# Mean squares of seven attention and recurrent heads, summed along the free axis with tokens on partitions

## The chip, the core and the metric

The kernel runs on one core of a Trainium2 chip. The metric is the device time of one execution in microseconds (us). Beside the times there is one profiled execution, taken by the hardware profiler. Its engines are PE (TensorE's matmuls; PEld are its weight loads), DVE (VectorE), ACT (ScalarE), POOL (GpSimd) and SP (which issues transfers). L96 is line 96 of the kernel before.

## The reference, cut to what matters

One layer of an encoder trunk on 512 tokens of width 1024, in float32: a norm, one wide input projection, three branches (pooling, differential attention with four heads, a bidirectional gated recurrence with four heads), gates, an output projection, a second norm, a SwiGLU feed-forward network (FFN) of 2816 hidden columns, a final norm. The change lies where a head's output, 512 tokens by 128 channels, is normalised:

```python
def rms_norm(x, g):
    y = xf * lax.rsqrt(jnp.mean(xf * xf, axis=-1, keepdims=True) + NORM_EPS)
    return (y * g).astype(x.dtype)
# attention, each of 4 heads
o = rms_norm(o, gain) * (1.0 - lambda_init)
# recurrence, each of 4 heads
o = rms_norm((o_f + o_b), gain).reshape(B, S, REC_WIDTH)
return o * jax.nn.silu(g)
```

The mean goes over a head's 128 channels, so there is one factor per token and head.

## The kernel before

**Arithmetic.** Products of float32 tensors are made from two parts each, a rounded one ("hi", fp32r) and its remainder ("lo"), as hi x hi + hi x lo + lo x hi. `split_w` (L185) makes the parts of a weight tile: ScalarE writes whi, VectorE wlo. The recurrence and the norms use plain float32 matmuls, which TensorE runs as two passes each; transposes (L104) take one.

**Stages.** The input is normalised and transposed to hT (channels on partitions, tokens along the free axis). Then come the recurrent heads, the attention heads, the gates and branch projections, the output projection, the FFN, and the last output product, which is made of plain products and of seven block products.

**Order.** The order of TensorE's instructions is written out by a planner, `Pipe` (L39). Every head is a stream (`rec_scan`, `att_head`), and one further stream, `jobs`, holds the projections. A stream yields ("w", t, slack): what follows it is to be issued no earlier than t us on the planner's own clock, which every matmul moves on by a fixed price (L93 to L105). Meanwhile the other streams' matmuls are issued. TensorE takes its instructions in that order and waits when an input isn't ready. The orders of the other engines are chosen by the framework from its own estimate of time.

**A head's norm.** Heads are worked with channels on partitions: o_ps in PSUM is 128 channels x 512 tokens. `head_norm` (L692 to L717) squares it on ScalarE (sqo, L697), copies it scaled by the gain (og, L698), and after a wait of 1.3 us takes the sum over partitions on TensorE: four float32 matmuls with a block of sqo as the stationary operand and one column of 1/128 as the moving one (L702), which leaves 128 tokens x 4 in PSUM. VectorE adds the epsilon (L153; attention, whose outputs are not yet divided by their softmax sums, multiplies by r0 twice before, L708 to L710), GpSimd raises to the power -0.5 (L147). After a further wait of 3.55 us four transposes of the broadcast column (L716) turn the factor back to the form of og, and VectorE multiplies (L1014 or L1160). A recurrent head also multiplies by its silu gate sg (L1013). The result is split into y_hi and y_lo. Tiles in PSUM come from two or three buffers for each of the names mm, rc and tp.

**Layout.** SBUF is given out by pools, one behind the other from the left: const, wraw (raw weights), wsp (the split weights whi and wlo, slots of 4352 bytes in each partition, 17 x 256), small, and then hTp with hT and all later pools: the attention tiles, the forms (sums of input blocks for products with fewer multiplications), h2 (the second norm's hT), the FFN's tiles wss (split sums shi and slo) and lw. The y arenas and a few others come from the right end. `small` reserves five slots of 32 bytes for each of its names: ss, rstd, ms, rso, mx, co, mo and ss2, 1280 bytes in all. Its end is where hT begins. The code places tiles by small distances: h2 stands behind a pad of 192 bytes (L1816), lw too (L1846), and `split_w` has a skip, by which whi and wlo begin 64 or 192 bytes into their slot:

```python
hi, lo = ((wpool or wsp).tile([P, n if wpool else 1088], F32R, name=name)[:, k:k + n]
```

Weights of 512-column products have no skip (but for a few branch projections, where it is 64), those of the gate pairs and of the first three fronts 64, and those of the value projections, where whi is the moving operand and hT the stationary one, 192. The FFN works in column pairs, seven products of 12 passes each with 256 columns; three take whi and four take shi.

Of the kernel before, what the change touches and what calls it, by code (L numbers as in the profile page):

```python
# [11 lines left out]
F32 = mybir.dt.float32  # L12
F32R = mybir.dt.float32r
U8 = mybir.dt.uint8
AF = mybir.ActivationFunctionType
ALU = mybir.AluOpType
PSUM = bass.MemoryType.PSUM

P = 128
S = 512  # L20
D = 1024
NB = S // P
KT = D // P
HEADS = 4
FFN = 2816
FT = FFN // P
EPS = 1e-6
# [55 lines left out]
def encoder_kernel(ctx: ExitStack, tc: tile.TileContext, x, norm1_g, w_in, pool_w, pool_scale,  # L83
# [3 lines left out]
    nc = tc.nc  # L87
# [7 lines left out]
    def mm(out_, lhsT, rhs, start, stop, chain=False):  # L95
        i = nc.tensor.matmul(out_, lhsT=lhsT, rhs=rhs, start=start, stop=stop, skip_group_check=chain)  # L96
        tc.keep_in_program_order(i)
        n = 1
        for d in rhs.shape[1:]:
            n *= d  # L100
        pipe.t += max(0.107, n * 0.0004167 + 0.002) if rhs.dtype == F32R else max(0.216, n * 0.001667 + 0.004)

    def transpose(out_, in_, idn):
        tc.keep_in_program_order(nc.tensor.transpose(out_, in_, idn))  # L104
        pipe.t += 0.108  # L105
# [11 lines left out]
    small = ctx.enter_context(pool("small", 5))  # L117
    psum = ctx.enter_context(pool("psum", 3, space=PSUM))

    def bank(name, shape=(P, 512)):  # L120
        return psum.tile(list(shape), F32, name=name, bufs=2 if name == "tp" else 3)
# [7 lines left out]
    ident = const.tile([P, P], F32, name="ident")  # L129
    make_identity(nc, ident)  # L130
    fixed = const.tile([P, 2], F32, name="fixed")
    onesD, minus1 = fixed[:, 0:1], fixed[:, 1:2]
    nc.vector.memset(onesD, 1.0 / P)
    nc.vector.memset(minus1, -1.0)
    mhalf = const.tile([P, 8], F32, name="mhalf")
    nc.vector.memset(mhalf, -0.5)
# [2 lines left out]
    gain_a = const.tile([P, 1], F32, name="gain_a")  # L139
# [4 lines left out]
    gain_r = vcol[:, 13:14]  # L144

    def pow_mhalf(dst, src):
        return nc.gpsimd.tensor_tensor(out=dst, in0=src, in1=mhalf[:, :src.shape[1]], op=ALU.pow).ins  # L147

    def rsqrt_eps(dst, mean):

        ms = small.tile([P, 8], F32, name="ms")[:, :mean.shape[1]]
        eng = nc.vector if mean.space == PSUM else nc.gpsimd
        eng.tensor_scalar(out=ms, in0=mean, scalar1=1.0, scalar2=EPS, op0=ALU.mult, op1=ALU.add)  # L153
        return pow_mhalf(dst, ms)

    LAST, FF = {}, {}
# [434 lines left out]
    ps = bank("mm")  # L591
# [13 lines left out]
    ps = bank("mm")  # L605
# [17 lines left out]
    last = first_split((on_act, on_dve))  # L623
# [65 lines left out]
        nc.vector.tensor_copy(out=masks, in_=maskf)  # L689
    st0.close()  # L690

    def head_norm(o_ps, tmp, gain, r0=None, bufs=2, slack=0.0):  # L692


        og = tmp.tile([P, S], F32, name="og", bufs=bufs)
        sq = tmp.tile([P, S], F32, name="sqo", bufs=bufs)
        nc.scalar.activation(out=sq, in_=o_ps, func=AF.Square)  # L697
        nc.scalar.activation(out=og, in_=o_ps, func=AF.Copy, scale=gain)  # L698
        yield ("w", 1.3, slack)
        sp = bank("tp")  # L700
        for b in range(NB):
            mm(sp[:, b:b + 1], sq[:, b * P:(b + 1) * P], onesD, True, True)  # L702
        r = small.tile([P, NB], F32, name="rso")
        if r0 is None:
            rsqrt_eps(r, sp[:, 0:NB])
        else:
            m = small.tile([P, NB], F32, name="mo")
            nc.vector.tensor_tensor(out=m, in0=sp[:, 0:NB], in1=r0, op=ALU.mult)  # L708
            nc.vector.tensor_tensor(out=m, in0=m, in1=r0, op=ALU.mult)
            nc.vector.tensor_scalar(out=m, in0=m, scalar1=EPS, scalar2=None, op0=ALU.add)  # L710
            pow_mhalf(r, m)
            nc.vector.tensor_tensor(out=r, in0=r, in1=r0, op=ALU.mult)
        yield ("w", 3.55, slack)
        rb = bank("tp")
        for b in range(NB):
            transpose(rb[:, b * P:(b + 1) * P], r[:, b:b + 1].to_broadcast([P, P]), ident)  # L716
        return og, rb  # L717
# [195 lines left out]
    def rec_scan(h):  # L913
# [30 lines left out]
        n = 1  # L944
# [54 lines left out]
                nc.vector.scalar_tensor_tensor(out=own, in0=st[:, 3 * d + prev, :], scalar=total, in1=ps[:, j, :],  # L999
                                               op0=ALU.mult, op1=ALU.add)  # L1000
        yield ("w", 2.4 if h < 3 else 1.6, slack)
        ps = bank("rc")
        for b in range(NB):
            o = ps[:, b * P:(b + 1) * P]
            mm(o, vs[b], pt[:, b, :], True, False)
            for d in range(2):
                if 0 <= b - 1 + 2 * d < NB:
                    j = b - 1 if d == 0 else b
                    mm(o, st[:, 3 * d + j, :], kq[:, 1 - d, b * P:(b + 1) * P], False, b == (0 if d else 3) or d == 1)
        mark(f"O{h}")  # L1010
        og, rbp = yield from head_norm(ps, rt, gain_r, slack=slack)
        yield ("e", f"G{h}", 0.0)
        nc.vector.tensor_tensor(out=og, in0=og, in1=sgs.pop(h), op=ALU.mult)  # L1013
        nc.vector.tensor_tensor(out=og, in0=og, in1=rbp, op=ALU.mult)  # L1014
        nc.scalar.copy(out=y_rec[0][:, h, :], in_=og)
        nc.vector.tensor_tensor(out=y_rec[1][:, h, :], in0=og, in1=y_rec[0][:, h, :].bitcast(F32), op=ALU.subtract)

# [72 lines left out]
    def att_head(h):  # L1090
        if h:
            yield ("e", f"QK{h - 1}", 0.0)
        yield ("e", f"AF{h}", 7.0 if h > 1 else 6.0)
        t = att.pop(h)
        at, (vh, vl), aT, y_attn = ATT["at"], ATT["v"], ATT["aT"], ATT["y"]
        strip = ATT["strip"].tile([P, 896], F32, name="strip")
        nc.sync.dma_start(out=strip, in_=c_dist[h])
        zz = at.tile([P, NB, 2], F32, name="zz")
        rr = at.tile([P, NB], F32, name="rr")
        probs = {}  # L1100

        def scores(i):
            bs = slice(i * P, (i + 1) * P)
            mx = small.tile([P, 2], F32, name="mx")
            ex = []
            for c in range(2):
                ps = bank("rc")
                mm(ps, t[f"q{c}"][:, bs], t[f"k{c}"], True, False)
                mm(ps, t[f"q{c}"][:, bs], t[f"l{c}"], False, True)
                s = at.tile([P, S], F32, name=f"s{c}")  # L1110

                nc.vector.tensor_tensor_reduce(out=s, in0=strip[:, 384 - P * i:896 - P * i], in1=ps, scale=1.0,  # L1112
                                               scalar=3.0e38, op0=ALU.add, op1=ALU.min, accum_out=mx[:, c:c + 1])
                nc.scalar.activation(out=s, in_=s, func=AF.Exp, scale=-1.0, bias=mx[:, c:c + 1],  # L1114
                                     accum_out=zz[:, i, c:c + 1])
                ex.append(s)

            co = small.tile([P, 2], F32, name="co")
            zn, co = co[:, 0:1], co[:, 1:2]
            nc.gpsimd.tensor_tensor(out=zn, in0=zz[:, i, 0:1], in1=nlam, op=ALU.mult)  # L1120
            nc.gpsimd.tensor_tensor(out=co, in0=zz[:, i, 1:2], in1=minus1, op=ALU.pow)
            nc.gpsimd.tensor_tensor(out=co, in0=co, in1=zn, op=ALU.mult)
            nc.vector.scalar_tensor_tensor(out=ex[0], in0=ex[1], scalar=co, in1=ex[0], op0=ALU.mult, op1=ALU.add)
            probs[i] = ex[0]

        def turn(i):
            bs = slice(i * P, (i + 1) * P)
            p = probs.pop(i)
            pt = bank("tp", (P, NB, P))
            for k in range(NB):  # L1130
                transpose(pt[:, k, :], p[:, k * P:(k + 1) * P], ident)
            nc.scalar.copy(out=aT[0][:, :, bs], in_=pt)
            nc.vector.tensor_tensor(out=aT[1][:, :, bs], in0=pt, in1=aT[0][:, :, bs].bitcast(F32), op=ALU.subtract)

        scores(0)
        for i in range(NB):
            yield ("w", 1.6 + (0.7 if i == 0 else 0.0))
            if i + 1 < NB:
                scores(i + 1)
            else:  # L1140
                mark(f"QK{h}")
            yield ("w", 2.4 + (1.0 if i + h == 0 else 0.0), 0.0)
            if h and i == 0:
                yield ("e", f"PV{h - 1}", 0.0)
            turn(i)
        mark(f"T{h}")
        nc.vector.reciprocal(out=rr, in_=zz[:, :, 0])
        yield ("e", "VA", 1.5)
        yield ("w", 1.5)
        ps = bank("rc")  # L1150
        es = slice(h * P, (h + 1) * P)
        terms = [(vh, aT[0]), (vl, aT[0]), (vh, aT[1])]
        for i, (a, r) in enumerate(terms):
            for k in range(NB):
                mm(ps, a[:, k, es], r[:, k, :], i == 0 and k == 0, i == 2 and k == NB - 1)
            yield
        mark(f"PV{h}")
        og, rbp = yield from head_norm(ps, at, gain_a, rr, 1, 6.0 if h < HEADS - 1 else 0.0)
        mark(f"AN{h}")
        nc.vector.tensor_tensor(out=og, in0=og, in1=rbp, op=ALU.mult)  # L1160
        nc.scalar.copy(out=y_attn[0][:, h, :], in_=og)
        nc.vector.tensor_tensor(out=y_attn[1][:, h, :], in0=og, in1=y_attn[0][:, h, :].bitcast(F32),
                                op=ALU.subtract)
# [733 lines left out]
```

## Time and profile before

| | us |
|---|---|
| median of 3 runs | 871.92 (871.59 to 872.09) |
| the profiled execution, its own time | 871.81 |
| its span, first to last instruction | 870.0 |
| TensorE matmuls busy | 862.4 |
| TensorE weight loads busy | 786.1 |
| VectorE busy | 659.2 |
| ScalarE busy | 448.7 |
| GpSimd busy | 37.1 |

How to read the rows of the profile: a group's row gives line, engine, operation, output<-inputs by the program's names, shape, xcount, then busy time and mean ns of one, then idle time of the engine before it and what ended it. Matmuls are pipelined, so that a pass's own duration is longer than the distance to the next; the pace is read from starts. A timeline row gives start, length, engine, line, operation and count; a row of the chain of waits gives start, length, engine, output, line and count; a row by windows gives the stretch, its length, then busy time and count of PE, PEld, DVE, ACT and POOL, the granted clock, the share and rate of transfers.

### The profile page before, as it was taken

Reading aid. Unit: us, or ns where it says so; the run is one execution under the profiler, and the core shown is the slowest. Engines: PE = TensorE matmul, PEld = TensorE weight load, DVE = VectorE, ACT = ScalarE, POOL = GpSimd, SP = SyncE. Lnnn points to the kernel's source line nnn. Section 1 sums busy time; section 2 is a strip of 40 time slices with the busy share of each in tenths; the row PEclk is TensorE's granted clock in tenths of the full one; section 3 lists DMA queues with packets and bytes.
Section 4 is the critical chain, followed back from the end, with each engine's and each line's share of the span. In section 5 each row is a group of like instructions: output and inputs, shape, how many; then the busy total and the mean of one; then the engine's idle time right before and its main releaser. Section 6 shows DMA issues by size and latency. Waiting matters only on the chain.

```text
span 870.0 us, 14113 instructions
## 1 busy us (share of the span) xinstructions
PE 862.4 (99%) x5713; PEld 786.1 (90%) x5713; DVE 659.2 (76%) x979; ACT 448.7 (52%) x721; POOL 37.1 (4%) x83
## 2 busy tenths in 40 slices
PE   9999999999999999999999999999999999999997
PEld 8989998888988888899999998999999999988886
DVE  6779644845757888987776756988888888847996
ACT  6644343435757664563354425655555655533563
POOL 2000000000102220000000001000000000000001
PEclk9999999999999999999999999999999999999999
DMA  8330113024133321343332840344433433355002
GB/s 245 98 122 25 50 49 121 25 74 151 43 95 90 90 68 49 97 146 98 97 98 97 288 124 1 85 112 128 114 98 108 136 98 99 121 194 192 2 1 98
DMA packets 115694, 87.54 MB, mean 101 GB/s; under 512 B 3862, under 2 KB 104748, under 8 KB 115628
## 3 DMA queue, kind: packets, MB, share of 16 engines
q1 hardware_dynamic: 115036, 85.57, 32.2%
q8 instruction: 45, 0.74, 0.4%
q10 hardware_dynamic: 592, 1.05, 0.3%
q14 instruction: 21, 0.17, 0.1%
HBM read 84.52 MB, written 2.10 MB: 100 GB/s over the span
## 4 chain that ended last, share of the span: by engine, by line
PE 98%; issue 1%; DMA 0%; DVE 0%; POOL 0%; ACT 0%; POOLq 0%
PE mm L96 65%; PE rc L96 28%; PE tp L96 3%; PE tp L104 2%; DMA xin<-in_x_dram 0%; PE rc L104 0%; DVE hrow L502 0%; POOL rstd L147 0%; ACT silu L1479 0%; ACT x L1503 0%; DVE x L1472 0%; DVE x L1481 0%; PE mm L104 0%; POOLq L1892 0%; POOL ms L153 0%
## 5 line engine op out<-in xcount | busy, mean ns | idle before, releaser
L191 ACT CAST whi<-raw 128x1024 fp32r<-128x1024 f32 (+1 forms) x134 | 127.5, 959 | 140.7 <-PE mm L96 95.2
L192 DVE TENSOR_TENSOR wlo<-raw,whi 128x1024 fp32r<-128x1024 f32 (+1 forms) x134 | 147.8, 1106 | 50.9 <-ACT whi L191 41.3
L96 PE MATMUL mm<-hT_hi,whi 128*128 128x512 f32 (+1 forms) x344 | 81.3, 370 | 0.0
L96 PE MATMUL mm<-hT_hi,wlo 128*128 128x512 f32 (+1 forms) x344 | 80.0, 368 | 0.0
L96 PE MATMUL mm<-hT_lo,whi 128*128 128x512 f32 (+1 forms) x344 | 78.8, 367 | 0.0
L96 PEld LDWEIGHTS mm<-hT_hi,whi 128*128 128x128 f32 x344 | 59.2, 188 | 10.3 <-ACT hT_hi L515 0.2
L96 PEld LDWEIGHTS mm<-hT_lo,whi 128*128 128x128 f32 x344 | 59.1, 188 | 9.8
L96 PEld LDWEIGHTS mm<-hT_hi,wlo 128*128 128x128 f32 x344 | 58.8, 188 | 9.5
L318 DVE TENSOR_TENSOR slo<-sums,shi 128x1024 fp32r<-128x1024 f32 x54 | 65.7, 1217 | 0.0
L316 ACT CAST shi<-sums 128x1024 fp32r<-128x1024 f32 x54 | 56.8, 1052 | 4.1 <-DVE sums L280 3.3
L276 DVE TENSOR_TENSOR sums<-raw 128x1024 f32<-128x1024 f32 x27 | 32.9, 1218 | 1.2 <-DMA raw<-in_w_in_dram 1.2
L96 PE MATMUL mm<-y_arena,whi 128*128 128x512 f32 x128 | 32.7, 394 | 0.0
L96 PE MATMUL mm<-whi,y_arena 128*128 128x256 f32 (+1 forms) x192 | 32.1, 317 | 0.0
L96 PE MATMUL rc<-kq,kc 128*128 128x128 f32 x224 | 30.4, 284 | 0.0
L96 PEld LDWEIGHTS rc<-kq,kc 128*128 128x128 f32 x224 | 29.2, 191 | 1.1
L961 DVE TENSOR_TENSOR kq<-kq,pyr 128x256 f32<-128x256 f32 x48 | 18.2, 420 | 15.8 <-PE rc L96 15.8
L96 PEld LDWEIGHTS mm<-whi,y_arena 128*128 128x128 f32 x192 | 27.9, 189 | 2.6
L929 ACT COPY kc<-kq 128x512 f32<-128x512 f32 x28 | 18.6, 667 | 21.6 <-DVE kq L955 8.2
L1114 ACT ACTIVATE s<-s,mx 128x512 f32<-128x512 f32 x32 | 23.0, 719 | 10.9 <-DVE mx L1112 10.2
L96 PEld LDWEIGHTS mm<-y_arena,whi 128*128 128x128 f32 x128 | 23.7, 188 | 5.1
L1413 DVE TENSOR_TENSOR g<-mm,g 128x256 f32<-128x256 f32 x21 | 8.9, 424 | 23.9 <-PE mm L96 23.4
L96 PE MATMUL mm<-fhi,shi 128*128 128x256 f32 x168 | 25.9, 276 | 0.0
(409 smaller groups left out, 2053.5 us busy)
## 6 DMA issues: line engine op xcount, KB each, us to landing
raw<-in_w_in_dram SPq DMA_DIRECT2D x44, 512.0 KB, 4.2
raw<-in_w_ffn_in_dram SPq DMA_DIRECT2D x44, 512.0 KB, 4.1
raw<-in_w_in_dram SPq DMA_DIRECT2D x8, 1024.0 KB, 5.2
raw<-in_w_ffn_out_dram SPq DMA_DIRECT2D x7, 1024.0 KB, 4.8
raw<-in_w_out_dram SPq DMA_DIRECT2D x4, 1024.0 KB, 10.1
xin<-in_x_dram SPq DMA_DIRECT2D x4, 512.0 KB, 4.6
raw<-in_w_up_rec_dram SPq DMA_DIRECT2D x2, 1024.0 KB, 7.6
raw<-in_w_up_pool_dram SPq DMA_DIRECT2D x2, 1024.0 KB, 5.0
```

Source lines behind the costliest of these rows:

```text
L96: i = nc.tensor.matmul(out_, lhsT=lhsT, rhs=rhs, start=start, stop=stop, skip_group_check=chain)
L104: tc.keep_in_program_order(nc.tensor.transpose(out_, in_, idn))
L191: LAST["whi"] = nc.scalar.copy(out=hi, in_=view).ins
L192: LAST["wlo"] = nc.vector.tensor_tensor(out=lo, in0=view, in1=hi.bitcast(F32), op=ALU.subtract).ins
L276: nc.vector.tensor_tensor(out=strided(sums, 0, [[2 * half, 2], [1, half]]), in0=strided(self.raw, 0, [[3 * half, 2], [1, half]]), in1=stri ...
L316: nc.scalar.copy(out=hi, in_=view)
L318: on_dve = nc.vector.tensor_tensor(out=lo, in0=view, in1=hi.bitcast(F32), op=ALU.subtract).ins
L929: nc.scalar.copy(out=strided(kc, 0, [[2 * n, S // (2 * n)], [n, 2], [1, n]]), in_=strided(kq, 2 * S, [[2 * n, S // (2 * n)], [S + n, 2], [ ...
L961: nc.vector.tensor_tensor(out=xv, in0=xv, in1=tv, op=ALU.mult)
L1114: nc.scalar.activation(out=s, in_=s, func=AF.Exp, scale=-1.0, bias=mx[:, c:c + 1], accum_out=zz[:, i, c:c + 1])
L1413: on_dve = nc.vector.tensor_tensor(out=c["g"], in0=c["x"], in1=c["g"], op=ALU.add).ins
```

## The change

A recurrent head's output is now formed with tokens on partitions: the operands of its output matmuls are swapped. `token_sums` squares on ScalarE and sums along the free axis on VectorE; the factor follows with `rsqrt_eps`, VectorE scales the output, and after one wait of 4.6 us four transposes turn it to channels on partitions. One VectorE step multiplies by gain and gate. The first three attention heads transpose their copied output, and the squares and sums are taken from the transposed blocks in PSUM; the small products by r0 go to GpSimd. The last attention head keeps its four one-column matmuls. The gain moves from the copy to the last product. `small` gets tiles of two new names, sso and rr2.

```diff
-    onesD, minus1 = fixed[:, 0:1], fixed[:, 1:2]
-    nc.vector.memset(onesD, 1.0 / P)
+    ones, minus1 = fixed[:, 0:1], fixed[:, 1:2]
+    nc.vector.memset(ones, 1.0)
...
+    def token_sums(o, tmp, bufs=2):
+        sq = tmp.tile([P, NB, P], F32, name="sqo", bufs=bufs)
+        ss = small.tile([P, NB], F32, name="sso")
+        nc.scalar.activation(out=sq, in_=o, func=AF.Square)
+        nc.vector.tensor_reduce(out=ss, in_=sq, op=ALU.add, axis=mybir.AxisListType.X)
+        return ss
...
-    def head_norm(o_ps, tmp, gain, r0=None, bufs=2, slack=0.0):
+    def head_norm(o_ps, tmp, r0, wait, bufs=2, slack=0.0, last=False):
         og = tmp.tile([P, S], F32, name="og", bufs=bufs)
-        sq = tmp.tile([P, S], F32, name="sqo", bufs=bufs)
-        nc.scalar.activation(out=sq, in_=o_ps, func=AF.Square)
-        nc.scalar.activation(out=og, in_=o_ps, func=AF.Copy, scale=gain)
-        yield ("w", 1.3, slack)
-        sp = bank("tp")
+        if last:
+            sq = tmp.tile([P, S], F32, name="sqo", bufs=bufs)
+            nc.scalar.activation(out=sq, in_=o_ps, func=AF.Square)
+        nc.scalar.copy(out=og, in_=o_ps)
+        rr = small.tile([P, NB], F32, name="rr2")
+        nc.gpsimd.tensor_tensor(out=rr, in0=r0, in1=r0, op=ALU.mult)
+        yield ("w", 1.2, slack)
+        turned = bank("tp", (P, NB, P))
         for b in range(NB):
-            mm(sp[:, b:b + 1], sq[:, b * P:(b + 1) * P], onesD, True, True)
+            bs = slice(b * P, (b + 1) * P)
+            if last:
+                mm(turned[:, 0, b:b + 1], sq[:, bs], ones, True, True)
+            else:
+                transpose(turned[:, b, :], og[:, bs], ident)
+        if last:
+            sums = small.tile([P, NB], F32, name="sso")
+            nc.vector.tensor_copy(out=sums, in_=turned[:, 0, 0:NB])
+        else:
+            sums = token_sums(turned, tmp, bufs)
+        m = small.tile([P, NB], F32, name="mo")
+        nc.gpsimd.tensor_tensor(out=m, in0=sums, in1=rr, op=ALU.mult)
+        nc.gpsimd.tensor_scalar(out=m, in0=m, scalar1=1.0 / P, scalar2=EPS, op0=ALU.mult, op1=ALU.add)
...
+        pow_mhalf(r, m)
+        nc.gpsimd.tensor_tensor(out=r, in0=r, in1=r0, op=ALU.mult)
+        yield ("w", wait, slack)
...
-            mm(o, vs[b], pt[:, b, :], True, False)
+            mm(o, pt[:, b, :], vs[b], True, False)
...
-        og, rbp = yield from head_norm(ps, rt, gain_r, slack=slack)
+        o = rt.tile([P, NB, P], F32, name="og")
+        sums = token_sums(ps, rt)
+        nc.scalar.copy(out=o, in_=ps)
+        r = small.tile([P, NB, 1], F32, name="rso")
+        rsqrt_eps(r[:, :, 0], sums, P)
+        nc.vector.tensor_tensor(out=o, in0=o, in1=r.to_broadcast([P, NB, P]), op=ALU.mult)
+        yield ("w", 4.6, slack)
+        turned = bank("tp")
+        for b in range(NB):
+            transpose(turned[:, b * P:(b + 1) * P], o[:, b, :], ident)
         yield ("e", f"G{h}", 0.0)
-        nc.vector.tensor_tensor(out=og, in0=og, in1=sgs.pop(h), op=ALU.mult)
-        nc.vector.tensor_tensor(out=og, in0=og, in1=rbp, op=ALU.mult)
+        og = sgs.pop(h)
+        nc.vector.scalar_tensor_tensor(out=og, in0=turned, scalar=gain_r, in1=og, op0=ALU.mult, op1=ALU.mult)
...
-        og, rbp = yield from head_norm(ps, at, gain_a, rr, 1, 6.0 if h < HEADS - 1 else 0.0)
+        og, rbp = yield from head_norm(ps, at, rr, 4.8 if h < HEADS - 1 else 3.5, 1, 6.0 if h < HEADS - 1 else 0.0, h == HEADS - 1)
         mark(f"AN{h}")
-        nc.vector.tensor_tensor(out=og, in0=og, in1=rbp, op=ALU.mult)
+        nc.vector.scalar_tensor_tensor(out=og, in0=og, scalar=gain_a, in1=rbp, op0=ALU.mult, op1=ALU.mult)
```

More of the change, by code (lines that the diff above doesn't have):

```diff
@@ L147, in pow_mhalf, with rsqrt_eps @@
         return nc.gpsimd.tensor_tensor(out=dst, in0=src, in1=mhalf[:, :src.shape[1]], op=ALU.pow).ins
-    def rsqrt_eps(dst, mean):
+    def rsqrt_eps(dst, mean, n=1):
         ms = small.tile([P, 8], F32, name="ms")[:, :mean.shape[1]]
-        eng = nc.vector if mean.space == PSUM else nc.gpsimd
-        eng.tensor_scalar(out=ms, in0=mean, scalar1=1.0, scalar2=EPS, op0=ALU.mult, op1=ALU.add)
+        eng = nc.vector if mean.space == PSUM or n > 1 else nc.gpsimd
+        eng.tensor_scalar(out=ms, in0=mean, scalar1=1.0 / n, scalar2=EPS, op0=ALU.mult, op1=ALU.add)
         return pow_mhalf(dst, ms)
@@ L690, in encoder_kernel @@
     st0.close()
-    def head_norm(o_ps, tmp, gain, r0=None, bufs=2, slack=0.0):
-        og = tmp.tile([P, S], F32, name="og", bufs=bufs)
-        sq = tmp.tile([P, S], F32, name="sqo", bufs=bufs)
-        nc.scalar.activation(out=sq, in_=o_ps, func=AF.Square)
-        nc.scalar.activation(out=og, in_=o_ps, func=AF.Copy, scale=gain)
-        yield ("w", 1.3, slack)
-        sp = bank("tp")
-        for b in range(NB):
-            mm(sp[:, b:b + 1], sq[:, b * P:(b + 1) * P], onesD, True, True)
-        r = small.tile([P, NB], F32, name="rso")
[L704 to L713, printed above, removed]
+    def token_sums(o, tmp, bufs=2):
[4 more added lines that the diff above has]
+        return ss
@@ L1001, in rec_scan @@
         yield ("w", 2.4 if h < 3 else 1.6, slack)
-        ps = bank("rc")
+        ps = bank("rc", (P, NB, P))
         for b in range(NB):
-            o = ps[:, b * P:(b + 1) * P]
-            mm(o, vs[b], pt[:, b, :], True, False)
+            o = ps[:, b, :]
+            mm(o, pt[:, b, :], vs[b], True, False)
             for d in range(2):
@@ L1008, in rec_scan @@
                     j = b - 1 if d == 0 else b
-                    mm(o, st[:, 3 * d + j, :], kq[:, 1 - d, b * P:(b + 1) * P], False, b == (0 if d else 3) or d == 1)
+                    mm(o, kq[:, 1 - d, b * P:(b + 1) * P], st[:, 3 * d + j, :], False, b == (0 if d else 3) or d == 1)
         mark(f"O{h}")
-        og, rbp = yield from head_norm(ps, rt, gain_r, slack=slack)
+        o = rt.tile([P, NB, P], F32, name="og")
[8 more added lines that the diff above has]
+            transpose(turned[:, b * P:(b + 1) * P], o[:, b, :], ident)
         yield ("e", f"G{h}", 0.0)
-        nc.vector.tensor_tensor(out=og, in0=og, in1=sgs.pop(h), op=ALU.mult)
-        nc.vector.tensor_tensor(out=og, in0=og, in1=rbp, op=ALU.mult)
+        og = sgs.pop(h)
+        nc.vector.scalar_tensor_tensor(out=og, in0=turned, scalar=gain_r, in1=og, op0=ALU.mult, op1=ALU.mult)
         nc.scalar.copy(out=y_rec[0][:, h, :], in_=og)
```

## The prediction

> **What bounds the kernel now.** I read the page's busy shares and granted clock first, then its chain of waits, then the waits of TensorE alone, then busy time by stage.
>
> ```profile
> span 870.0 us, 14113 instructions
> PE 862.4 (99%) x5713; PEld 786.1 (90%) x5713; DVE 659.2 (76%) x979; ACT 448.7 (52%) x721; POOL 37.1 (4%) x83
> PEclk9999999999999999999999999999999999999999
> PE 98%; issue 1%; DMA 0%; DVE 0%; POOL 0%; ACT 0%; POOLq 0%
> ```
>
> The span is TensorE from end to end, at full granted clock. The list of its waits holds one entry, at the very start:
>
> ```profile
> PE mm L96 <- POOL ident masks.py:199: 1.3, 1, 1.3
> ```
>
> The two stages that the change edits (recurrent heads, 120 to 204 us; attention heads, 204 to 335 us) show it busy in every microsecond:
>
> ```profile
> 120.00:204.00 84.00, 84.00 (x486) 73.58 (x485) 46.09 (x84) 33.03 (x52) 4.00 (x4) 1.00 0.23 70
> 204.00:335.00 131.00, 131.00 (x726) 112.95 (x725) 92.69 (x190) 81.92 (x154) 23.13 (x52) 1.00 0.29 89
> ```
>
> So an edit counts by the TensorE time it adds or removes, by a TensorE wait it creates, and by anything that alters the pace of the 5713 passes. The third decides here.
>
> **Removed and added on TensorE.** A float32 matmul is two passes: 64 passes for the 8 heads with 4 one-column products each.
>
> ```profile
> L96 PE MATMUL tp<-fixed,sqo x64: 164/250/250, 124.6 to 331.7; 128*128 128x1 f32 x64
> ```
>
> What they take is read from weight loads, first start to the next group's first start:
>
> ```profile
> 124.49 0.97 PEld L96 LDWEIGHTS tp<-fixed,sqo 128*128 128x128 f32 x8
> 125.39 0.30 PEld L96 LDWEIGHTS rc<-pt,v_rec 128*128 128x128 f32 x2
> ...
> 131.56 1.98 PEld L96 LDWEIGHTS tp<-fixed,sqo 128*128 128x128 f32 x16
> 133.46 0.30 PEld L96 LDWEIGHTS mm<-hT_hi,wlo 128*128 128x128 f32 x2
> ```
>
> 0.90 us for one head, 1.90 us for two: 0.90 to 0.95 us a head, about 112 to 119 ns a pass, although one column is computed. The chain prices four transposes at 0.44 us:
>
> ```profile
> 130.12 0.44 PE tp L104 x4
> ```
>
> Seven heads lose their eight passes: 7 x 0.925 = 6.5 us. The four recurrent heads swap the four transposes of the broadcast scale for four of the scaled output, which is even. The three attention heads gain four transposes each: 3 x 0.44 = 1.3 us. Swapping the operands of the output matmuls keeps their count and size: even. Sum: **-5.2 us** (-5.0 to -5.3).
>
> The Trainium skill prices this otherwise ("TensorE: Matmul & The Clock Gate", "Wait — 56ns, not 53.3ns?"): starts of small matmuls are never closer than about 25 ns. By that, as an estimate, eight passes are 0.2 us, seven heads 1.4 us, the transposes eat the gain, and the total below would be 5 us higher. The rows show 112 ns and more per pass, so the measured price stands.
>
> **Other engines.** These costs are hidden as long as the transposes find their input ready.
>
> ```profile
> L697 ACT ACTIVATE sqo<-rc x8: 575/597/599, 123.5 to 329.4; 128x512 f32<-128x512 f32 x8
> ...
> L1013 DVE TENSOR_TENSOR og<-og,sg x4: 684/693/693, 124.7 to 194.7; 128x512 f32<-128x512 f32 x4
> ...
> L147 POOL TENSOR_TENSOR rso<-ms,mhalf x4: 1006/1009/1015, 126.0 to 196.4; 128x4 f32<-128x4 f32 x4
> L712 DVE TENSOR_TENSOR rso<-rso,rr x4: 163/164/164, 266.0 to 333.7; 128x4 f32<-128x4 f32 x4
> ...
> L192 DVE TENSOR_TENSOR wlo<-raw,whi 128x1024 fp32r<-128x1024 f32 x28 | 34.1, 1223 | 19.3 <-ACT whi L191 10.8 <-PE mm L96 6.3 <-ACT kT L982 1.2
> L1121 POOL TENSOR_TENSOR co<-zz,fixed 128x1 f32<-128x1 f32 x16 | 11.2, 702 | 12.4 <-ACT s L1114 12.4
> L1122 POOL TENSOR_TENSOR co<-co 128x1 f32<-128x1 f32 x16 | 3.6, 226 | 1.1
> ```
>
> A recurrent head must now run square 0.60, reduction (not shown; the nearest 128x512 row, 0.69), small VectorE step 0.16, power on GpSimd 1.01, scaling 0.69: 3.15 us, and some 0.7 us of hand-overs (estimate, 0.1 us each with the matmul's tail) make 3.9 us against the 4.6 us that the planner leaves. Attention after its transposes: 0.60 + 0.69 + 1.01 + four small GpSimd products near 0.23 (the row of co), with hand-overs 3.8 us against 4.8. The next head's three co steps sit in the same GpSimd queue (0.7 + two near 0.25, about 1.2 us), and one weight split holds VectorE 1.22 us. When one of these falls in front, a head overruns by up to 0.5 us; TensorE, in order, then waits with every matmul queued behind. Seven heads: 0 to +4 us; I take **+0.5**, near the low end, because single collisions are mostly covered by the 0.7 to 1 us of room. VectorE's extra reductions (7 x 0.69 = 4.8 us) lie under a stage in which it is idle 38 of 84 us.
>
> **What moves: the layout.** This is the term that counts. `small` reserves five slots of 32 bytes for every name used in it, and stands in front of all later left-hand pools. It has eight names now: 1280 bytes, five times 256. The change brings two more ("sso", "rr2"): 320 bytes, so everything behind (hT, the attention tiles, the forms, h2, the FFN tiles) moves by 64 modulo 256 against `wsp`, which holds the split weights whi/wlo, and against the right-hand arenas. No pad follows the move.
>
> The trace shows that this distance sets TensorE's pace. Take moving address minus stationary address, modulo 256, as tile sizes, pads and skips of the code give it. For 512 columns: hT over unskipped whi is at 0, y_arena over whi with the 64-byte skip is at 192, and h2 (padded by 192) over the first FFN weights is at 192:
>
> ```profile
> 59.59 5.47 PE mm L96 x24
> ...
> 364.92 5.59 PE mm L96 x24
> ...
> 548.34 5.59 PE rc L96 x24
> ```
>
> 228 ns at 0, 233 ns at 192, same size and clock. For 256 columns it is the reverse: h2 over whi of `wsp` in the FFN is at 192, and in the last product, whose whi lies in the pool `lw` behind a pad of its own, at 0:
>
> ```profile
> 600.96 0.62 PE L96 MATMUL rc<-h_hi,whi 128*128 128x256 f32 x4
> 601.42 0.62 PE L96 MATMUL rc<-h_lo,whi 128*128 128x256 f32 x4
> ...
> 859.86 0.64 PE L96 MATMUL rc<-h_hi,wlo 128*128 128x256 f32 x4
> 860.34 0.64 PE L96 MATMUL rc<-h_hi,whi 128*128 128x256 f32 x4
> ```
>
> Start to start over four passes: 0.46 us (a longer run, 1.36 us for 12 in the chain, gives 113 ns) against 0.48 us, 120 ns.
>
> ```profile
> 601.13 1.36 PE rc L96 x12
> ```
>
> Now the passes that change place, from the groups by shape:
>
> ```profile
> L96 PE MATMUL mm<-hT_hi,whi 128*128 128x512 f32 x264 | 69.2, 396 | 0.0
> ...
> L96 PE MATMUL mm<-whi,hT_lo 128*128 128x256 f32 x128 | 17.7, 280 | 0.0
> ...
> L96 PE MATMUL mm<-fhi,whi 128*128 128x256 f32 x84 | 12.9, 276 | 0.0
> ...
> L96 PE MATMUL mm<-hT_hi,whi 128*128 128x256 f32 x80 | 12.1, 284 | 0.0
> ...
> L96 PE MATMUL mm<-whi,shi 128*128 128x512 f32 x30 | 11.7, 389 | 0.0
> ```
>
> - 256 columns, 192 to 0: the FFN's three of seven products per column pair that take whi (three groups of 84, three terms each: 756), the same three of the gate pairs (288), the first three fronts (144): 1188 x 6.7 ns = **+8.0 us**. Both paces are shown.
> - 256 columns, whi moving over hT, 192 to 128: three terms of 128 = 384. 128 is not shown in bulk; between the paces 113 and 120 it costs 0 to 2.6 us; I take +2.3, as a step of 128 keeps the parity of 0.
> - 512 columns, 0 to 64: three terms of 264 = 792 over hT, with attention's y and the last products about 960. 64 is not shown in bulk; the other odd multiple, 192, is 5 ns slower (5.59 less 5.47 over 24). Bounds 0 and twice that: 0 to 9.6 us; I take 5 ns, **+4.8**.
> - 512 columns, whi over shi in the plain output products, 0 to 192: 240 x 5 ns = +1.2. About 60 passes go from 192 to 0: -0.3.
>
> Layout: +16.0 us (8.9 to 21.1). The split partner tiles that move together (shi, forms, attention's q and k) keep their pace.
>
> **Sum** against the profiled execution (871.81 us, span 870.0, within 0.11 of the median of 871.92): 871.8 - 5.2 + 0.5 + 16.0 = **883.1 us**. Its own range: 871.8 - 5.3 + 8.9 = 875.4 to 871.8 - 5.0 + 4 + 21.1 = 891.9.
>
> **Rivals.**
> (1) *Faster:* placement does not matter, and the two paces above have other causes (those rows lie in different stages). It decides if the FFN's passes stay at 113 ns after the move. Then 871.8 - 5.2 + 0.5 = 867.1 us. Against it: the same pair h_hi, whi runs at both paces at one granted clock, and two sizes react. The Trainium skill speaks for it ("TensorE: Matmul & The Clock Gate", "Step-by-step: what each phase is for"): the moving operand and the weight load have independent read ports, so loading does not cost the running matmul. The rows at 113 and 120 ns disagree. Chance 0.12.
> (2) *No difference:* no layout price, but late transposes: each of seven heads overruns by one collision of 0.5 to 0.6 us, 867 + 4 = 871 us. For it: only 0.7 us of room. Against: VectorE's idle time. Chance 0.04.
> (3) *Only the shown offsets cost:* 64 and 128 are as good as 0 and 192, giving 875.4 us; it lies in the forecast's range.
> (4) Layout price and stalls of more than 4 us: above 892. Chance 0.04.
>
> **Chances.** The forecast holds 0.80. About 0.2% (1.7 us) is what a measurement here can tell from no change. Faster 0.13, within 0.2% 0.04, slower 0.83. The range 873 to 891 leaves out the fast case, the neutral one and the far tail.
>
> **What would show it.** In the profile after: the one-column passes of seven heads gone, 5713 - 56 + 12 = 5669 passes; the FFN's runs over whi at 1.44 us per 12 and those over shi still at 1.36, so a column pair takes 9.76 us where it took 9.52; runs of 24 over hT at about 5.6 us; the recurrent and attention stages not shorter by 5 us. If runs over whi stay at 1.36, the layout step is wrong and (1) holds. TensorE waits above 1 us at the transposes of the scaled output would show (2).

## The result, and the profile after

The change makes the kernel slower: 884.5 us median (884.17 to 884.66) against 872.0, a ratio of 1.0147 with a 95% interval of 1.0134 to 1.016. The forecast was 883.1 us, with a range of 873 to 891.

The page after has the same picture as before: TensorE is the span, at full clock.

```profile
span 882.4 us, 14040 instructions
PE 874.7 (99%) x5669; PEld 795.5 (90%) x5669; DVE 662.2 (75%) x971; ACT 449.4 (51%) x721; POOL 39.5 (4%) x99
PEclk9999999999999999999999999999999999999999
```

TensorE has the 5669 passes that were forecast, 44 fewer than before, and is busy for 12.3 us longer. So the passes are slower, and the chain of waits shows which. One column pair of the FFN before (columns: start, length, engine, output, line, count):

```profile
598.41 2.72 PE mm L96 x24
...
602.49 1.36 PE mm L96 x12
...
607.93 2.72 PE mm L96 x24
```

One column pair after the change:

```profile
601.60 2.88 PE mm L96 x24
604.48 1.44 PE rc L96 x12
605.92 1.41 PE mm L96 x12
607.33 1.41 PE rc L96 x12
608.75 1.41 PE mm L96 x12
610.16 1.42 PE rc L96 x12
611.58 2.88 PE mm L96 x24
```

From the first row to the last, 601.60 to 611.58, the pair takes 9.98 us; before it took 9.52 (598.41 to 607.93). The three products over whi (one row of 24 passes, one of 12) pay 120 ns a pass, as forecast. The four over shi, 12 passes each, pay 118 ns; 113 had been forecast for them, since shi and what streams over it moved together.

Elsewhere after the change, a value projection (46 passes with whi or wlo moving over hT), a front projection of 512 columns over hT, a branch projection with the skip of 64, and a plain output product:

```profile
83.96 5.46 PE mm L96 x46
...
60.02 5.51 PE mm L96 x24
...
363.33 5.60 PE mm L96 x24
...
768.22 2.80 PE tp L96 x12
```

The first was 5.23 us, so it lost 5 ns a pass. But the value projections had two paces before, and a later one, at 5.42, rose only to 5.47:

```profile
83.38 5.23 PE mm L96 x46
...
97.48 5.42 PE mm L96 x46
```

The second of the four rows was 5.47 before: only 1.7 ns a pass. The third, whose operands did not move against each other, has 5.60 where it had 5.59. The fourth runs at 233 ns.

The waits of TensorE's weight loads show what the new steps of the heads cost there:

```profile
PEld tp L104 <- issue: 0.4, 2, 0.2
PEld rc L96 <- ACT aT_hi L1158: 0.4, 1, 0.4
...
PEld tp L104 <- POOL rso L729: 0.3, 1, 0.3
```

Late inputs are some 0.3 us for the transposes of the factor, and 0.4 us behind the probability tiles.

### The profile page after: what moved, and what is told of

Same layout as the page of the kernel before. It is cut to its first block, busy times and chain, and to the rows that moved or that the text cites. A ratio compares the mean times of both kernels' runs of the same rounds, so it can differ in the third digit from the quotient of the medians.

```text
span 882.4 us, 14040 instructions
## 1 busy us (share of the span) xinstructions
PE 874.7 (99%) x5669; PEld 795.5 (90%) x5669; DVE 662.2 (75%) x971; ACT 449.4 (51%) x721; POOL 39.5 (4%) x99
## 4 chain that ended last, share of the span: by engine, by line
PE 98%; DMA 1%; ACT 0%; issue 0%; DVE 0%; SPq 0%; POOLq 0%; POOL 0%
PE mm L96 65%; PE rc L96 28%; PE tp L96 2%; PE tp L104 2%; DMA raw<-in_w_in_dram 1%; PE rc L104 0%; ACT hT_hi L515 0%; ACT whi L191 0%; SPq L569 0%; ACT silu L1505 0%; ACT x L1529 0%; DVE x L1498 0%; DVE x L1507 0%; POOLq L1918 0%; POOL rstd L147 0%
## 5 line engine op out<-in xcount | busy, mean ns | idle before, releaser
L978 DVE TENSOR_TENSOR kq<-kq,pyr 128x256 f32<-128x256 f32 x48 | 18.2, 421 | 16.8 <-PE rc L96 16.7
L96 PE MATMUL mm<-flo,shi 128*128 128x256 f32 x168 | 26.6, 281 | 0.0
```

What stands on the lines that cost most here:

```text
L978: nc.vector.tensor_tensor(out=xv, in0=xv, in1=tv, op=ALU.mult)
```

## The experiments

Two theories stood at the start. **Layout:** the cost comes from the 320 bytes that two new names add to `small`. **Work:** it comes from the change's own steps and order. Each time below is a median, beside runs of the kernel before on the same chip (871.5 to 871.6 us).

### The change without the move, and the move without the change

The first run takes the slots of two old names for the new tiles; the two old names are in use only elsewhere in the kernel.

```diff
-        ss = small.tile([P, NB], F32, name="sso")
+        ss = small.tile([P, NB], F32, name="ss2")
...
-        rr = small.tile([P, NB], F32, name="rr2")
+        rr = small.tile([P, NB], F32, name="ss")
...
-            sums = small.tile([P, NB], F32, name="sso")
+            sums = small.tile([P, NB], F32, name="ss2")
```

> The whole change, but its two new names in small take the slots of two old ones (ss2 and ss), so that hT and all behind it stand where they stood before. Layout theory: the cost is the move by 320 bytes; 872.0 - 5.2 + 0.5 = about 867 us (866 to 869), the FFN at 9.52 us per column pair. Rival, the work and order of the change itself (late transposes, more VectorE and GpSimd work): 884 to 885 us as with the change.

The second adds unused bytes to the kernel before.

```diff
+    pad(small, 320, "small_a")
     psum = ctx.enter_context(pool("psum", 3, space=PSUM))
```

> The kernel before with 320 unused bytes in small and nothing else. Layout theory: 872.0 + (884.5 - 867) = 887 to 890 us, with the FFN at 9.97 us per column pair as after the change. Rival, the change's own work: 872 us, within 0.2%.

Measured: **866.82 us** without the move (ratio 0.9943, 0.9928 to 0.9958), **888.44 us** with the move alone (1.0195, 1.0178 to 1.0212). The order of TensorE's instructions is the same in the first as with the change. The work theory falls: the change saves 4.8 us, and the move costs 16.8 us on the kernel before and 17.7 us on the changed one (884.5 less 866.8; 17.3 when each is first taken against its own runs of the kernel before). The chain of the first shows the FFN at its old pace, that of the second at the new one. Without the move:

```profile
640.95 2.72 PE mm L96 x24
643.67 1.36 PE rc L96 x12
```

With the move alone:

```profile
645.66 2.88 PE mm L96 x24
648.54 1.44 PE rc L96 x12
649.98 1.41 PE mm L96 x12
```

### Is it the move, or its size modulo 256?

Three more moves of the kernel before, made with the same line and another number of bytes.

> The kernel before with 256 unused bytes in small. If the distance counts modulo 256, nothing changes: 871 to 873 us, FFN at 9.52 us per column pair. Rival, any move of the left pools against the weights or the right-hand arenas costs (or the distance counts modulo 512 or more): clearly above 873 us.

> The kernel before with 128 unused bytes in small: the FFN's 256-column passes over whi go from distance 192 to 64, the 512-column passes over hT from 0 to 128. If what counts is the odd or even multiple of 64, nothing much changes: 871 to 873 us. If every distance has its own price, the total moves by 3 us or more, most likely up.

> The kernel before with 192 unused bytes in small: 256-column passes over whi go from 192 to 128, 512-column ones over hT from 0 to 192, where the kernel before shows 233 ns. If 128 is as slow as 0 for 256 columns, the sum is 1188 x 6.7 ns + 960 x 5 ns + 384 x 6 ns for the values + 6 us for shi runs that inherit a slower pace: 872 + 21 = 893 us. If 128 is as quick as 192 for 256 columns: 872 + 5 + 1 = about 878 us.

Measured: 256 bytes **871.60 us** (1.0, 0.9991 to 1.001); 128 bytes **879.29 us** (1.0088, 1.0074 to 1.0102); 192 bytes **885.18 us** (1.0155, 1.0141 to 1.0169). The distance counts modulo 256. The rule by odd and even multiples of 64 falls for 512 columns: with 128 bytes, the runs over hT are slow although 128 is an even multiple. For 256 columns it holds so far: the FFN's runs over whi, now at 64, are as quick as they were at 192. The value projections, at 64 too, take 5.42 us for 46 passes, 118 ns, so 64 has the slower pace as well. The rows are a front projection's, a value projection's and the FFN's:

```profile
59.90 5.59 PE mm L96 x24
...
84.06 5.42 PE mm L96 x46
...
706.64 1.36 PE rc L96 x12
708.00 2.72 PE mm L96 x24
```

With 192 bytes, whi lies at 128 for 256 columns and pays 118 to 119 ns; shi, which moved along, is quick here:

```profile
60.17 5.61 PE mm L96 x24
...
702.59 1.36 PE rc L96 x12
703.95 2.84 PE mm L96 x24
706.79 1.43 PE rc L96 x12
```

So the prices are, in ns a pass, by moving less stationary address modulo 256:

| distance | 512 columns | 256 columns |
|---|---|---|
| 0 | 228 (5.47 us for 24) | 120 (1.44 for 12) |
| 64 | 230 (5.51) | 113 or 118 (1.36; 5.42 for 46) |
| 128 | 233 (5.59) | 118 to 119 (2.84 for 24, 1.43 for 12) |
| 192 | 234 (5.61) | 113 or 118 (1.36, 1.41) |

The run with 192 bytes came out 8 us under its forecast of 893. Part of the miss is shi, which did not slow down (6 us had been put in for it); the rest wasn't taken apart.

### Why the runs over shi slowed although nothing between their operands moved

Theory A says that they inherit a slower pace from the 120 ns runs before them; theory B, that they are slow at their new place. The experiment gives the FFN's whi and wlo a skip of 64 in the changed kernel, so that only their distance returns to 192.

```diff
-    pairs = {j: pair_parts(j, *ffn_cols(j), after.get(j, (None,) * 4)) for j in range(1, FT)}
+    pairs = {j: pair_parts(j, *ffn_cols(j), after.get(j, (None,) * 4), 64) for j in range(1, FT)}
```

> The change with the FFN's whi and wlo begun 64 bytes into their slots: their distance to h2 and the forms is 192 modulo 256 again, while shi, slo, h2 and the forms stay where the change put them. The whi runs go back from 1.44 to 1.36 us per 12 passes in both readings. Theory A, the shi runs at 1.41 inherit their slower pace from the 1.44 runs that precede them: shi runs go back to 1.36 too, the column pair to 9.52, the total to 884.5 - 20 x 0.45 = 875 to 876 us. Theory B, the shi runs are slower because of where shi and the forms now stand: they stay at 1.41, the pair at 9.73, the total about 879.5 us.

Measured: **876.72 us** (1.0057, 1.0042 to 1.0072), which is 7.8 us less than the change. Theory B falls, since shi reaches 113 ns at its new place. And since only whi and wlo moved here, while the tiles that stream over them stayed where the change put them, the 120 ns came from the distance between the two and not from the place of the streaming tile. But the quick pace does not hold from the start: the first three pairs run at 1.41 throughout, whi included, and the quick pace comes in the fourth pair.

```profile
580.41 2.83 PE mm L96 x24
583.24 1.41 PE rc L96 x12
584.65 0.47 PE tp L96 x2
585.12 0.46 PE mm L96 x4
585.58 0.47 PE tp L96 x2
586.05 0.92 PE mm L96 x8
586.97 1.36 PE rc L96 x12
```

Between 1.41 and 1.36 stand two pairs of 512-column passes (PE tp, x2 each). Both kernels have them in the fourth column pair; nothing reads what they write. The changed kernel itself shows theory A at the same place: after these passes its runs over shi are quick too, and the next runs over whi, at 120 ns, bring them back to 1.41. Of the changed kernel:

```profile
586.17 0.47 PE tp L96 x2
...
587.55 1.36 PE rc L96 x12
...
591.63 2.88 PE mm L96 x24
...
595.95 1.41 PE mm L96 x12
```

The next two runs take them out, from the kernel above and from the one without the move.

```diff
-            if j == 4:
-                unread(part)
...
-                if (j, n) == (4, 1):
-                    unread(part)
```

> The kernel of the run ffn_skip without the four extra 512-column passes in the FFN's fourth column pair, whose outputs nothing reads; in that run the first three pairs took 9.89 us and, from these passes on, every pair 9.52. Theory, a run of 256-column passes at distance 192 has two paces and keeps the one it is in until something throws it over, here the four wide passes: without them all pairs stay at 9.89, so 876.7 - 0.9 (the four passes) + 16 x 0.37 = about 881.7 us. Rival, the pace of the first pairs had another cause (weights just loaded, the forms just made) that ends by itself: pairs at 9.52 from the fourth on, 875.8 us.

> The kernel of the run layout_back without the same four passes. There the FFN is at 9.52 us per pair from the first. Theory of two paces that persist: nothing throws it over, all pairs at 9.52, 866.8 - 0.9 = 865.9 us. Rival, the four passes are needed to hold the quick pace: 866 + 16 x 0.37 = 872 us. An execution that enters the FFN in the slow pace would show 9.89 in all pairs and about 872 us.

Measured: **881.76 us** (1.0116, 1.0101 to 1.0132) and **865.97 us** (0.9934, 0.9917 to 0.995). In the first, the FFN's last column pairs still run slow; the second is quick throughout. The last pairs of the first:

```profile
745.92 1.41 PE mm L96 x12
...
748.75 2.83 PE mm L96 x24
```

The second, where the four passes stood:

```profile
580.51 1.36 PE mm L96 x12
...
583.23 2.72 PE mm L96 x24
```

So 256-column passes at distance 192 have two paces, 113 and 118 ns. A run stays in the one that it is in for over a thousand passes, and 512-column passes can throw it over. The FFN of this last kernel relies on entering in the quick pace. All four of its executions lay between 865.88 and 866.14 us, but nothing in it enforces that. It is the fastest version found, 0.66% under the kernel before.

### The two parts of the change, unmoved

The recurrent part alone: every attention head keeps its one-column matmuls, in the form that the change leaves to the last head.

```diff
-        og, rbp = yield from head_norm(ps, at, rr, 4.8 if h < HEADS - 1 else 3.5, 1, 6.0 if h < HEADS - 1 else 0.0, h == HEADS - 1)
+        og, rbp = yield from head_norm(ps, at, rr, 3.5, 1, 6.0 if h < HEADS - 1 else 0.0, True)
```

> The unmoved layout with the recurrent part alone; all four attention heads keep four one-column matmuls in the form that the change leaves to the last head. By the price of passes: 4 heads x 0.925 us off: 871.6 - 3.7 = 868 us (867.5 to 868.5). Rival, the gain sits mainly in attention or in order: 870 us or more.

The attention part alone: recurrent heads with the old output matmuls and the old norm, its one column now 1.0 and the 1/128 in the VectorE step.

```diff
-            mm(o, pt[:, b, :], vs[b], True, False)
+            mm(o, vs[b], pt[:, b, :], True, False)
...
+        og, rbp = yield from norm_columns(ps, rt, gain_r, slack)
```

> The unmoved layout with the attention part alone; recurrent heads keep their one-column matmuls and transposes of the factor. By the price of passes: 3 x (0.925 - 0.44) = 1.5 us off: 870.1 us (869.6 to 870.8). Rival, late inputs take it back (a chain of 3.8 us in a room of 4.8, and GpSimd shared with the next head): 871.5 us or above. Rival, a one-column pass is nearly free and a transpose is not: 873 us.

Measured: recurrent **867.88 us** (0.9956, 0.9943 to 0.9968), 3.7 us saved, as worked out. Attention alone **871.64 us** (0.9997, 0.9988 to 1.0006), no gain. Where its gain went is read from first starts of three tiles' matmuls: the scores, the pool mix (both ends of the attention stage), and the FFN's forms. Of the kernel before:

```profile
L96 PE MATMUL rc<-k,q x32: 387/392/401, 214.7 to 316.0; 128*128 128x512 f32 x32
...
L96 PE MATMUL rc<-dhi,pwhi x4: 389/389/389, 342.4 to 364.1; 128*128 128x512 f32 x4
...
L96 PE MATMUL mm<-fhi,shi x168: 276/276/281, 553.8 to 748.2; 128*128 128x256 f32 x168
```

Of the attention part alone:

```profile
L96 PE MATMUL rc<-k,q x32: 387/389/401, 214.4 to 315.1; 128*128 128x512 f32 x32
...
L96 PE MATMUL rc<-dhi,pwhi x4: 389/389/389, 341.1 to 362.8; 128*128 128x512 f32 x4
...
L96 PE MATMUL mm<-fhi,shi x168: 276/276/281, 552.6 to 748.2; 128*128 128x256 f32 x168
```

From the first scores to the pool mix it was 127.7 us and is 126.7: 1.0 us saved, still there (1.2, with 0.3 us from the start) when the FFN begins. The FFN then takes 1.1 us longer and ends at nearly the same time. Its chain shows why; it entered in the slow pace and kept it until the four wide passes, three pairs at 9.89 instead of 9.52 us:

```profile
578.22 2.83 PE mm L96 x24
...
582.46 0.47 PE tp L96 x2
```

Its executions spread from 870.14 to 872.04 us, wider than those of any other kernel here. An entry in the quick pace would account for the low ones; that is not shown, as only one execution, of 871.79 us, was profiled.

## Why the prediction was right

The sign and the cause hold, and the time lies 1.4 us above the forecast. Two terms were mis-sized in opposite directions, by -3.2 and about +5.6 us; that they largely offset each other is luck.

- **Removed and added passes, -5.2 us.** Right in size: the change without the move saves 4.8 us with the 0.5 us of late inputs already in it, where -5.2 + 0.5 = -4.7 was forecast. The recurrent part gives 3.7 of 3.7 us. The price of 112 ns and more for a one-column pass holds: 3.7 us for 32 passes is some 115 ns. The Trainium skill ("TensorE: Matmul & The Clock Gate", "Wait — 56ns, not 53.3ns?") gives about 25 ns as a floor between the starts of small matmuls, which 115 ns does not contradict; taken as the price, it would have left an estimated 0.8 us to save there.
- **Late inputs, +0.5 us.** Of the right order: attention saves 1.0 us in its stage where 1.5 was priced, and the rows of waits show tenths of a microsecond. Rival (2) falls.
- **256 columns from 192 to 0, +8.0 us.** Right: 1.44 and 2.88 us, 120 ns, where whi is the stationary tile in the FFN and the gates.
- **256 columns, whi over hT, +2.3 us.** Somewhat high: 5.46 less 5.23 over 46 passes is 5 ns, so 384 x 5 = 1.9 us at most; the projection that was at 5.42 already lost 1 ns a pass. The argument by parity behind the chosen value is borne out for 256 columns: 128 takes 118 to 119 ns, near the 120 of 0.
- **512 columns from 0 to 64, +4.8 us.** The first term that was mis-sized. The step "the other odd multiple, 192, is 5 ns slower" took 64 to cost what 192 does; it costs 1.7 ns, about 960 x 1.7 = 1.6 us. For 512 columns parity does not hold: 64 is near 0, and 128 near 192.
- **Plain output products, +1.2 us.** 2.80 us for 12 passes is 233 ns. Without the move the chain has 227, so 240 passes cost 1.6 us:

```profile
774.24 2.72 PE tp L96 x12
```

- **"The split partner tiles that move together keep their pace."** Wrong, and the second mis-sized term, with a price of nothing. The FFN's 48 passes over shi per pair went from 113 to 118 ns: from 1.36 to 1.41 us per 12, in 20 pairs (the fourth is quick after the wide passes): 20 x 4 x 0.05 = 4.0 us. The gates have eight such groups, also at 1.41 in the chain after, some 1.6 us at the same rate (worked out, not measured alone). The tiles do keep their distance, but not their pace: the 120 ns runs between them throw them into the slower one.

Together the move was forecast at 16.0 us and measured at 17.7 us (17.3 by the other count above); the terms as sized here add up to 8.0 + 1.9 + 1.6 + 1.6 + 4.0 + 1.6 = 18.7 us, with the value term at its upper bound.

Rival (1), that placement does not matter, falls with the run that makes the move alone: here the pace of a running matmul depends on the distance between its moving and its stationary tile. The Trainium skill ("TensorE: Matmul & The Clock Gate", "Step-by-step: what each phase is for") says that loading the next weights takes no read bandwidth from the running matmul. What the prediction drew from it for this rival does not hold here; whether the weight load and the moving stream collide in reading is not shown. Rival (3) falls, as 256 columns at 128 do pay, but it was nearly right for 512 columns at 64; its 875.4 us leaves out the late inputs. Rival (4) did not come about.

## What to carry to other kernels

Where TensorE is busy throughout, count what an edit does to the addresses as well as what it does to the passes: ten small slots that no engine waits for cost more here than 44 removed passes gave. After adding a tile, compare the pace per pass of runs that the edit did not touch, as the chain of waits gives it (length over count), before looking for waits. To judge an edit's own worth, time it with the layout held still.

## What the runs showed that was not expected

- At one distance, 192, 256-column passes have two paces, 113 and 118 ns, and the pace persists: through 16 more column pairs (9.89 instead of 9.52 us each, 5.9 us) when nothing interrupts it. Two pairs of 512-column passes, 0.9 us, end it. In the changed kernel runs over whi at distance 0, 120 ns, put the runs over shi behind them into the slow pace; in the FFN of the kernel moved by 192 bytes, runs over whi at distance 128, 118 to 119 ns, do not. What starts the slow pace where no run at 120 ns stands just before, as in the first pairs of the attention part alone, stays open.
- The price by distance does not have the same order for the two widths: 0 is the best for 512 columns and the worst for 256.
- A move of 256 bytes is free to within 0.1%, and one of 128, which is smaller, costs 7.7 us.
